# Gates of two branches as seven half-block products, and pooling inputs by way of DRAM

## The chip, the cores and the metric

The kernel runs on one core of a Trainium2 chip. A core has TensorE (PE: matmuls, with a queue of weight loads of its own, PEld), VectorE (DVE), ScalarE (ACT), GpSimd (POOL) and SyncE (SP), whose queue issues all of this kernel's DMAs. The metric is the time of one execution on the device in microseconds (us), the median of several runs.

## The reference

One layer of a streaming encoder over 1152 tokens (1024 of a prompt, 8 x 16 of samples), width 1024, in float32: a gated feed-forward block, a mixer, and a second feed-forward block, each between norms. What matters here is the mixer:

```python
proj = xn @ w_in   # [pooling 512 | z 1024 | x/B/C 2048 | dt 16 | u 512 | v 512 | gates 3*1024]
ya = pool_mixer(xa)            # branch A: trailing-window means of 512 channels
yb = rms_norm(ssd(x, B, C, dt) * silu(z))   # branch B: state-space scan
yc = u * spatial_gate(layer_norm(v))        # branch C
gates = sigmoid(gate_cols)     # three gates of 1024 channels
merged = gates[0] * (ya @ wa) + gates[1] * (yb @ wb) + gates[2] * (yc @ wc)
out = merged @ w_out
```

The gates are thus three products of the normed input (1152 x 1024) with weights of 1024 x 1024, each followed by a sigmoid.

## The kernel before

Tokens are cut into 9 tiles of 128, and these into NCHK = 3 chunks of CH = 384. Channels lie on the 128 partitions. Every float32 operand of a large product is split into a high part (an ACT cast to the type float32r) and a low part (a DVE subtraction: `split`, L123), and each product is three matmuls (low x high, high x low, high x high: `mm3`, L203). `proj` (L209) makes one output tile of 128 channels x 384 tokens with 8 x 3 = 24 matmuls of 384 columns into a PSUM bank. `load_w` (L127) loads one 1024 x 128 weight column block (512 KB) into a staging buffer (three of them) and splits it into one of two buffers `w_hi`, `w_lo`.

The normed input of the mixer is held as `xT[c]`, high and low, for the three chunks. The stages follow each other in `trunk`:

- the first feed-forward block (`gate_up`, then `down`, with `tail`);
- eight units of filler for PE, four of them between the last transposes (L1167 to L1174). The filler is a generator, `gate_out(0)`: it makes gate A one output tile (column block j, chunk c) at a time, chunk 0 first, with a weight load for each, and stores it in DRAM (`gad`). `filler(k)` (L813) takes the next k units;
- `z_dt` (L530): z in four groups of 256 columns, nine tiles each, weights in two buffers (`wz`); the terms of dt behind the second group;
- `branch_c` (L607): loads of its norm vectors, biases and spatial weights (`gn_g`, `gn_b`, `bs`, `ws`: L613 to L627), then v in two halves; one filler unit and the transposes of the spatial weights (`turned`, L628, which begins with DVE's masked copy L630) stand ahead of the second half; then u;
- `branch_a` (L695): four groups of 128 channels. Each computes its pooling input for three chunks (72 matmuls, L722 to L729) into `x`, then sums in up to four steps on DVE and POOL in turn (L737), the difference `zz` (L741), three units of filler (in the last group all that are left, L750), and the group's small product (`pya`, L761);
- `merge_ac` (L775): for each of 8 column blocks j: gate C for three chunks (72 matmuls), multiplied into `acc` with the product of branch C (`pyw`, 36 matmuls); then gate A read back from DRAM (`sa`) and multiplied with the product of branch A (36 matmuls), POOL's sum, and a store to DRAM (`accd`);
- `ssd` (branch B, with gate B as filler), `finish`, the output projection and the second feed-forward block.

The feed-forward blocks already use a scheme with seven half-block products in place of eight (`operands` L263, `weights` L289, `prod` L321, `cell` L328). A 2 x 2 block product, with the input dimension halved and two column blocks against two token blocks, is made from seven products of sums of blocks: `weights` makes seven half blocks of 512 x 128 from two loaded columns with four subtractions on POOL and splits each into a buffer `w2`; `operands` does the like for the tokens; `cell` adds the products with DVE and ACT in PSUM banks and in x and y.

Instructions are put in order by a scheduler at build time: program order is the priority, and an instruction takes its place in its engine's queue, in order, when the scheduler expects its operands and a free buffer. At run time every queue runs strictly in order, SP's too, each instruction waiting for its semaphores. Buffers of a pool are shared out in program order, to whichever is free.

Of the kernel before, what the change touches and what calls it, by code (L numbers as in the profile page):

```python
# [18 lines left out]
P = 128  # L19
D = 1024  # L20
# [41 lines left out]
class Net:  # L62
# [75 lines left out]
    def load_wide(self, pool, w, c0, extra=None):  # L138

        nc = self.nc  # L140
        hi = pool.tile([P, 8, 272], F32R, name="wz_hi")
        lo = pool.tile([P, 8, 272], F32R, name="wz_lo")
# [146 lines left out]
    def weights(self, w, c_left, c_right, wp=None):  # L289

        nc = self.nc
        raw = []
        for c0 in (c_left, c_right):
            r = self.stage("wraw").rearrange("p (k c) -> p k c", k=KD)
            nc.sync.dma_start(r, w[:, c0 : c0 + P].rearrange("(k p) c -> p k c", p=P))
            raw.append(r)
        b11, b21 = raw[0][:, 0:4], raw[0][:, 4:8]
        b12, b22 = raw[1][:, 0:4], raw[1][:, 4:8]
        t1 = self.wtp.tile([P, 4, P], F32, name="wt")
        B = {}  # L300

        def out(name, raw):
            b = (wp or self.wp).tile([P, 2, 4, P], F32R, name="w2")
# [12 lines left out]
        op(b21, b21, t1)  # L316
        out("t4", b21)
        out("22", b22)
        return B

    def prod(self, ps, b, a, first):  # L321
# [173 lines left out]


class Mixer:
    def __init__(self, n, xT, yz_d, zs_d, acc_d, ga_d, gb_d, cum_d, last_d):
        self.n, self.nc, self.tc, self.io, self.xT = n, n.nc, n.tc, n.io, xT
        self.yz_d, self.zs_d, self.acc_d, self.ga_d, self.gb_d, self.cum_d, self.last_d = yz_d, zs_d, acc_d, ga_d, gb_d, cum_d, last_d  # L500
        self.w_in = self.io["w_in"][0]

    def masks(self, pool):
# [23 lines left out]
        self.strict_s = pool.tile([P, P], F32, name="strict_s")  # L527
        nc.gpsimd.tensor_tensor(self.strict_s, self.strict, bd, op=ALU.mult)

    def z_dt(self, pool):  # L530

        n, nc, io = self.n, self.nc, self.io
        dtb = n.spread(pool, io["ssm_dt_bias"][0], "dtb")
        self.dt = pool.tile([P, NT, HEADS], F32, name="dt")
        with self.tc.tile_pool(name="wz", bufs=2) as wz, self.tc.tile_pool(name="zt", bufs=3) as zt:
            for g in range(GROUPS):
                w = n.load_wide(wz, self.w_in, C_Z + 256 * g, C_DT if g == 0 else None)
                nn = 272 if g == 0 else 256
                for t in range(NT):
                    ps = n.psum("pz")  # L540
                    n.proj_tok(ps, t, self.xT, w, nn)
                    z = zt.tile([P, 256], F32, name="z")
                    nc.scalar.activation(z, ps[:, :256], AF.Silu)
                    nc.sync.dma_start(self.zs_d[t * P : (t + 1) * P, 256 * g : 256 * g + 256], z)
                    if g == 0:
                        nc.vector.tensor_tensor(self.dt[:, t, :], ps[:, 256:272], dtb, op=ALU.add)
                if g == 1:
                    self.dt_terms(pool, zt)

    def dt_terms(self, pool, tmp):  # L550
        n, nc, io = self.n, self.nc, self.io
# [52 lines left out]
        nc.vector.tensor_copy(el, tp[:HEADS, P : 2 * P].rearrange("p (b i) -> p b i", i=LSEQ)[:, :, LSEQ - 1])  # L604
        nc.sync.dma_start(self.last_d, el)

    def branch_c(self, pool):  # L607

        n, nc, tc, io = self.n, self.nc, self.tc, self.io
        self.yc = [pool.tile([P, 4, TOK], F32R, name=f"yc{i}") for i in range(2)]  # L610
        with tc.tile_pool(name="cc", bufs=1) as cc, tc.tile_pool(name="ct", bufs=3) as ct:
# [36 lines left out]
            with tc.tile_pool(name="wz", bufs=1) as wz:  # L648
                for half in range(2):
                    w = n.load_wide(wz, self.w_in, C_V + 256 * half)  # L650
                    if half == 1:
                        self.filler(1)
                        turned()
                    for t in range(NT):
                        ps = n.psum("pv")
                        n.proj_tok(ps, t, self.xT, w, 256)
                        nc.scalar.copy(vv[:, t, 256 * half : 256 * half + 256], ps[:, :256])
                        if half == 1:
                            self.layer_norm(ct, vv[:, t, :], gn_g, gn_b)
                            if t == 8:  # L660
                                nc.sync.dma_start(io["gmlp_v_s"][0].rearrange("b s c -> (b s) c"), vv[:, t, :])
# [33 lines left out]
    def branch_a(self, pool):  # L695
# [5 lines left out]
        with tc.tile_pool(name="pa", bufs=1) as pa:  # L701
# [15 lines left out]
            for g in range(4):  # L717
# [1 line left out]
                x = pa.tile([P, RAWP], F32, name="xa")  # L719
                nc.gpsimd.memset(x[:, :POOL_HIST], 0.0)  # L720
                nc.gpsimd.tensor_copy(sample(x)[:, :, :POOL_HIST], hT[:, g])
                for c in range(NCHK):  # L722
                    ps = n.psum("pxa")
                    n.proj(ps, w, self.xT[c])
                    if c < 2:
                        nc.scalar.copy(x[:, POOL_HIST + c * CH : POOL_HIST + (c + 1) * CH], ps[:, :CH])
                    else:
                        nc.scalar.copy(x[:, POOL_HIST + 2 * CH : sb], ps[:, : 2 * P])
                        nc.scalar.copy(sample(x)[:, :, POOL_HIST:], ps[:, 2 * P : CH].rearrange("p (b i) -> p b i", i=LSEQ))  # L729
                win = 2  # L730
                s = x
                for step in range(g + 1):
# [42 lines left out]
    def merge_ac(self):  # L775

        n, nc, tc, io = self.n, self.nc, self.tc, self.io
        with tc.tile_pool(name="mac", bufs=3) as mp, tc.tile_pool(name="macc", bufs=NCHK + 1) as mk:
            for j in range(KD):
                js = slice(j * P, (j + 1) * P)  # L780
                acc = [mk.tile([P, CH], F32, name="acc") for _ in range(NCHK)]
                wg = n.load_w(self.w_in, C_G + 2 * D + j * P, KD)
                wyc = n.load_w(io["w_branch_c"][0], j * P, 4)
                for c in range(NCHK):
                    cs = slice(c * CH, (c + 1) * CH)
                    s = mp.tile([P, CH], F32, name="sg")
                    self.gate(wg, self.xT[c], s)
                    ps = n.psum("pyw")
                    n.proj(ps, wyc, [v[:, :, cs] for v in self.yc], 4)
                    nc.vector.tensor_tensor(acc[c], s, ps[:, :CH], op=ALU.mult)  # L790
                wya = n.load_w(io["w_branch_a"][0], j * P, 4)
                for c in range(NCHK):
                    cs = slice(c * CH, (c + 1) * CH)
                    s = mp.tile([P, CH], F32, name="sa")
                    nc.sync.dma_start(s, self.ga_d[js, cs])
                    ps = n.psum("pyw")
                    n.proj(ps, wya, [v[:, :, cs] for v in self.ya], 4)
                    nc.vector.tensor_tensor(s, s, ps[:, :CH], op=ALU.mult)
                    nc.gpsimd.tensor_tensor(acc[c], acc[c], s, op=ALU.add)
                    nc.sync.dma_start(self.acc_d[js, cs], acc[c])  # L800
# [277 lines left out]
def trunk(ctx, tc, io):  # L1078
# [30 lines left out]
    with ExitStack() as c0:  # L1109
# [44 lines left out]
        with ExitStack() as c1:  # L1154
# [7 lines left out]
                tail(io["ffn1_post_g"][0], 0.5, lambda t: rows(io, t), at(h1), lambda t, h, xn: n.prenorm(t, h, gn, xT, xn)),  # L1162
            )
            m = Mixer(
                n, xT, dram("yz", [TOK, D]), dram("zs", [TOK, D]), dram("acc", [D, TOK]), dram("gad", [D, TOK]), dram("gbd", [D, TOK]), dram("cumd", [NT * HEADS, P]), dram("lastd", [HEADS, NSEQ])
            )
# [105 lines left out]
```

## Time and profile before

| | |
|---|---|
| median of 3 runs | 2885.55 us (2882.87 to 2886.64) |
| profiled execution | 2887.22 us, its span 2885.5 us |
| PE, PEld busy | 2797.2 us, 2635.4 us |
| DVE, ACT, POOL busy | 1366.8, 985.9, 767.3 us |
| DMA | 335.14 MB, mean 116 GB/s |

The span is the profiled part of one execution. An engine is busy while it works on an instruction; busy shares add over stages with different limits, so each stage is looked at by itself. The rows below give for an instruction its line, engine, operation, output and inputs, and in brackets how long its engine was idle before it and what ended that.

### The profile page before, as it was taken

To read this page: it belongs to the slowest core of one execution; us is meant where nothing else is said; L and a number is where in the kernel's file an instruction comes from. 1 tells how busy PE (TensorE), PEld (TensorE's weight loads), DVE (VectorE), ACT (ScalarE), POOL (GpSimd) and SP (SyncE) were. 2 spreads that over 40 slices of the span, in tenths; PEclk is the share of its full clock that TensorE was granted. 3 is DMA by queue.
4 is the path that set the end of the run, shared out by engine and by line. 5 is a ranking of instruction groups with operands and counts; after the bars stand their busy time and mean duration, and the time that the engine had idled before them with its cause. 6 is when DMAs were issued, how large, how long until landed. Compare 5 with 4: busy or idle time off the path is not lost. (4 is left out here: it accounts for less than half of the span.)

```text
span 2885.5 us, 43479 instructions
## 1 busy us (share of the span) xinstructions
PE 2797.2 (97%) x17310; PEld 2635.4 (91%) x17310; DVE 1366.8 (47%) x1989; ACT 985.9 (34%) x1720; POOL 767.3 (27%) x877
## 2 busy tenths in 40 slices
PE   6999999999999999999999999999989999999999
PEld 6999999888889999999998889998789999998887
DVE  7544443445643063322266676544564444445553
ACT  6322222344443112311134446523342222224442
POOL 3443343100010010111146676221233333330000
PEclk9999999999999999999999999999999999999999
DMA  4222221556654113332323446744122222226663
GB/s 128 69 80 77 73 69 55 170 189 212 214 148 133 49 44 92 101 94 86 108 66 101 116 107 176 225 136 152 66 94 81 69 73 70 83 74 220 222 215 108
DMA packets 331463, 335.14 MB, mean 116 GB/s; under 512 B 23150, under 2 KB 285538, under 8 KB 331261
## 3 DMA queue, kind: packets, MB, share of 16 engines
q1 hardware_dynamic: 331261, 332.37, 37.5%
q8 instruction: 136, 2.23, 0.3%
q14 instruction: 66, 0.54, 0.1%
HBM read 263.06 MB, written 69.25 MB: 115 GB/s over the span
## 5 line engine op out<-in xcount | busy, mean ns | idle before, releaser
L324 PE MATMUL pw<-A_s,w 128*128 128x288 f32 x4224 | 607.0, 299 | 17.0 <-ACT A_s L124 8.4
L324 PEld LDWEIGHTS pw<-A_s,w 128*128 128x128 f32 x4224 | 575.5, 191 | 25.0 <-ACT A_s L124 9.1
L206 PE MATMUL down<-wd,hh 128*128 128x512 f32 x2376 | 542.5, 390 | 4.0 <-ACT wd L124 3.1
L206 PEld LDWEIGHTS down<-wd,hh 128*128 128x128 f32 x2376 | 444.9, 188 | 98.5 <-ACT wd L124 4.1
L324 PE MATMUL pw<-A,w 128*128 128x288 f32 x3168 | 452.5, 296 | 8.1 <-DVE A L125 5.2
L324 PEld LDWEIGHTS pw<-A,w 128*128 128x128 f32 x3168 | 433.0, 190 | 9.3 <-DVE A L125 5.4
L206 PE MATMUL pgate<-xT,w_hi 128*128 128x384 f32 x1152 | 295.6, 338 | 0.0
L125 DVE TENSOR_TENSOR w<-wraw,w 128x512 fp32r<-128x512 f32 x220 | 180.4, 822 | 130.3 <-ACT w L124 130.0
L125 DVE TENSOR_TENSOR wd<-wdraw,wd 128x1024 fp32r<-128x1024 f32 x140 | 172.5, 1236 | 127.5 <-ACT wd L124 127.1
L206 PEld LDWEIGHTS pgate<-xT,w_hi 128*128 128x128 f32 x1152 | 209.4, 189 | 0.4
L206 PE MATMUL pgate<-xT,w_lo 128*128 128x384 f32 x576 | 196.9, 342 | 9.4 <-DVE w_lo L125 9.4
L206 PE MATMUL pxbc<-xT,w_hi 128*128 128x384 f32 x768 | 199.0, 339 | 0.0
L124 ACT CAST wd<-wdraw 128x1024 fp32r<-128x1024 f32 x140 | 146.6, 1051 | 141.9 <-PE down L206 90.6
L125 DVE TENSOR_TENSOR w_lo<-wraw,w_hi 128x1024 fp32r<-128x1024 f32 (+1 forms) x104 | 127.4, 1225 | 123.2 <-ACT w_hi L124 110.5
L124 ACT CAST w<-wraw 128x512 fp32r<-128x512 f32 x220 | 135.6, 619 | 62.3 <-PE pw L324 32.6
L163 POOL TENSOR_SCALAR post_r<-post_ss 128x1 f32<-128x1 f32 x27 | 8.3, 306 | 552.5 <-ACT junk L174 552.5
L375 POOL TENSOR_TENSOR wh<-wh,wy 128x288 f32<-128x288 f32 x88 | 82.3, 936 | 234.3 <-ACT wh L364 169.4
L206 PEld LDWEIGHTS pxbc<-xT,w_hi 128*128 128x128 f32 x768 | 140.8, 191 | 0.1
L206 PE MATMUL pxbc<-xT,w_lo 128*128 128x384 f32 x384 | 133.7, 348 | 0.0
L124 ACT CAST w_hi<-wraw 128x1024 fp32r<-128x1024 f32 (+1 forms) x104 | 102.4, 985 | 85.9 <-PE pyw L206 45.9
L349 ACT ACTIVATE wh<-pw 128x288 f32<-128x288 f32 x88 | 36.2, 411 | 276.2 <-PE pw L324 275.7
L341 DVE TENSOR_TENSOR wx<-wx,pw 128x288 f32<-128x288 f32 x176 | 79.7, 453 | 100.2 <-PE pw L324 99.6
(281 smaller groups left out, 4249.6 us busy)
## 6 DMA issues: line engine op xcount, KB each, us to landing
wdraw<-in_ffn_w_down_dram SPq DMA_DIRECT2D x132, 512.0 KB
wraw<-in_ffn_w_gu_dram SPq DMA_DIRECT2D x88, 512.0 KB
wraw<-in_w_in_dram SPq DMA_DIRECT2D x80, 512.0 KB
hff<-wh SPq DMA_DIRECT2D x88, 288.0 KB
hr<-hff SPq DMA_DIRECT2D x132, 192.0 KB
h<-fg SPq DMA_DIRECT2D x18, 512.0 KB
cumb<-cumd SPq DMA_DIRECT2D x36, 256.0 KB
h<-h SPq DMA_DIRECT2D x18, 512.0 KB
```

The lines of the kernel that those rows point to most:

```text
L124: self.last_hi = self.nc.scalar.copy(hi, raw)
L125: return (eng or self.nc.vector).tensor_tensor(lo, raw, hi.bitcast(F32), op=ALU.subtract)
L163: nc.gpsimd.tensor_scalar(r, ss[0], ss[1], eps, op0=ALU.add, op1=ALU.add)
L206: mm = self.nc.tensor.matmul(ps, lhsT=lhs[a], rhs=rhs[b], start=first and i == 0, stop=last and i == 2)
L324: self.nc.tensor.matmul(ps[:, :HCH], lhsT=b[:, x, k], rhs=a[:, y, k], start=first and k == 0 and i == 0, stop=k == 3 and i == 2, skip_grou ...
L341: nc.vector.tensor_tensor(o, i, b[k][:, :HCH], op=ALU.add)
L349: nc.scalar.activation(h[:, 0], b[2][:, :HCH], AF.Silu)
L375: nc.gpsimd.tensor_tensor(h[:, 1], h[:, 1], y, op=ALU.mult)
```

## The change

Gates A and C are no longer made as filler and in the merge. For chunks 0 and 1 they are made together, in a stage of their own between z and branch C, as eight pairs: column block j of gate A and column block j of gate C are the two columns, chunks 0 and 1 the two token blocks, and each pair takes seven products of 12 matmuls with 384 columns (`pair`). The sums of token blocks are made once, on POOL, in buffers of the pool `aux` (five in all), and split (`sums`). Both gates go to DRAM. The third chunk of both gates is the new filler of branches C and A (`gates_last`, 16 units, each with a weight load). The pooling inputs of chunks 0 and 1 become the filler behind the first feed-forward block (`xa_out`, 8 units with 4 weight loads) and go through DRAM; branch A computes only chunk 2 and loads the rest. Branch C takes two more units of filler ahead of v. The merge reads gate C from DRAM. The z weights alternate between two pools, one of which makes room for four buffers of the pairs' weights (`Wa`); the other three are in `Wb`. z goes through the pool `act` (three buffers).

```diff
     def prod(self, ps, b, a, first, n=HCH):
...
-                    ps[:, :HCH], lhsT=b[:, x, k], rhs=a[:, y, k], start=first and k == 0 and i == 0, stop=k == 3 and i == 2, skip_group_check=not first
+                    ps[:, :n], lhsT=b[:, x, k], rhs=a(y, k), start=first and k == 0 and i == 0, stop=k == 3 and i == 2, skip_group_check=not first
...
-    def z_dt(self, pool):
+    def z_dt(self, pool, sp, cg):
...
-        with self.tc.tile_pool(name="wz", bufs=2) as wz, self.tc.tile_pool(name="zt", bufs=3) as zt:
+        with self.tc.tile_pool(name="wzb", bufs=1) as wzb, self.tc.tile_pool(name="zt", bufs=3) as zt:
+            ca = ExitStack()
+            wza = n.pool(ca, "wza", 1, "right")
             for g in range(GROUPS):
-                w = n.load_wide(wz, self.w_in, C_Z + 256 * g, C_DT if g == 0 else None)
+                if g == 3:
+                    ca.close()
+                    wa = n.pool(cg, "Wa", 4, "right")
+                w = n.load_wide((wza, wzb)[g % 2], self.w_in, C_Z + 256 * g, C_DT if g == 0 else None)
+                if g == 2:
+                    self.sums(sp)
...
+    def sums(self, pool):
...
+        self.S = {k: pool.tile([P, 2, 4, CH], F32R, name=f"S{k}") for k in ("s1", "s3", "s2", "s4")}
+        for kp in range(2):
+            raw = {}
+            for t in range(2):
+                for k in range(2):
+                    ks = slice(4 * k + 2 * kp, 4 * k + 2 * kp + 2)
+                    r = raw[t, k] = n.aux("sraw")[:, : 2 * CH].rearrange("p (k c) -> p k c", k=2)
+                    nc.gpsimd.tensor_tensor(r, x[t][0][:, ks].bitcast(F32), x[t][1][:, ks].bitcast(F32), op=ALU.add)
...
+            def out(name, dst, a, b, op):
+                nc.gpsimd.tensor_tensor(dst, a, b, op=op)
+                n.split(dst, self.S[name][:, 0, ks], self.S[name][:, 1, ks])
...
+    def pair(self, c_left, c_right, left, right, wp):
...
+        B = n.weights(self.w_in, c_left, c_right, wp)
+        xy = n.aux("gw")
+        x, y = xy[:, :CH], xy[:, 512 : 512 + CH]
...
+        def put(ps, add, dst, c):
+            s = n.actp.tile([P, CH], F32, name="sgo", tag="act")
+            if add is None:
+                nc.scalar.activation(s, ps[:, :CH], AF.Sigmoid)
+            else:
+                nc.vector.tensor_tensor(s, add, ps[:, :CH], op=ALU.add)
+                nc.scalar.activation(s, s, AF.Sigmoid)
+            nc.sync.dma_start(dst[:, c * CH : (c + 1) * CH], s)
+
+        b1 = prod("11", "11")
+        nc.scalar.copy(x, b1[:, :CH])
+        b = prod("t2", "s2")
+        nc.vector.tensor_tensor(x, x, b[:, :CH], op=ALU.add)
+        b = prod("t3", "s3")
+        nc.vector.tensor_tensor(y, x, b[:, :CH], op=ALU.add)
+        b5 = prod("t1", "s1")
+        put(b5, y, right, 1)
+        put(prod("t4", "22"), y, left, 1)
+        prod("21", "12", b1)
+        put(b1, None, left, 0)
+        prod("22", "s4", b5)
+        put(b5, x, right, 0)
+
+    def gates_ac(self, wa, wb):
+        for j in range(KD):
+            js = slice(j * P, (j + 1) * P)
+            self.pair(C_G + j * P, C_G + 2 * D + j * P, self.ga_d[js], self.gc_d[js], lambda k: wa if k in ("11", "t1", "t2", "t3") else wb)
...
     def branch_c(self, pool):
...
                     w = n.load_wide(wz, self.w_in, C_V + 256 * half)
+                    if half == 0:
+                        self.filler(2)
...
     def branch_a(self, pool):
...
-                for c in range(NCHK):
-                    ps = n.psum("pxa")
-                    n.proj(ps, w, self.xT[c])
...
+                nc.sync.dma_start(x[:, POOL_HIST : POOL_HIST + 2 * CH], self.xa_d[g * P : (g + 1) * P])
+                ps = n.psum("pxa")
+                n.proj(ps, w, self.xT[2])
...
     def merge_ac(self):
...
-                wg = n.load_w(self.w_in, C_G + 2 * D + j * P, KD)
...
-                    self.gate(wg, self.xT[c], s)
+                    nc.sync.dma_start(s, self.gc_d[js, cs])
...
-            m.fill, m.filled = m.gate_out(0, m.ga_d), 0
+            m.fill, m.filled = m.xa_out(), 0
...
-            m.z_dt(mixc)
+            with tc.tile_pool(name="S", bufs=1) as sp, tc.tile_pool(name="wt", bufs=1) as n.wtp, ExitStack() as cg:
+                wa = m.z_dt(mixc, sp, cg)
+                m.gates_ac(wa, n.pool(cg, "Wb", 3))
+            m.fill, m.filled = m.gates_last(), 0
```

## Rows read from the trace of the kernel before

**Rows 1.** The page: busy time of the engines, and GB/s in 40 slices of the span.

```profile
PE 2797.2 (97%) x17310; PEld 2635.4 (91%) x17310; DVE 1366.8 (47%) x1989; ACT 985.9 (34%) x1720; POOL 767.3 (27%) x877
...
GB/s 128 69 80 77 73 69 55 170 189 212 214 148 133 49 44 92 101 94 86 108 66 101 116 107 176 225 136 152 66 94 81 69 73 70 83 74 220 222 215 108
```

**Rows 2.** The waits of PE from 820 to 1640 us.

```profile
PE pgate L206 <- DVE w_lo L125: 4.6, 4, 1.6
...
PE wsT L640 <- DVE ws L630: 3.8, 1, 3.8
```

**Rows 3.** PE's timeline where the fillers after the first stage wait longest.

```profile
848.23 0.44 PE L206 MATMUL pgate<-xT,w_lo 128*128 128x384 f32 x1 [1.59 <-DVE w_lo L125]
```

**Rows 4.** PE in windows around 1008 us: us, busy (count), clock, DMA, GB/s.

```profile
1008.00:1012.00 4.00, 2.78 (x11) 0.57 0.06 7
...
1012.00:1016.00 4.00, 4.00 (x23) 0.58 0.96 275
```

**Rows 5.** SP's timeline from 940 to 1010 us, its loads for branch C.

```profile
977.30 0.33 SPq L485 DMA_DIRECT2D gn_g<-in_gmlp_norm_g_dram  x1
...
978.62 16.51 SPq L618 DMA_DIRECT2D bs<-in_gmlp_bs_dram  x4
...
995.18 11.04 SPq L627 DMA_DIRECT2D ws<-in_gmlp_ws_dram  x8
```

**Rows 6.** Busy time in windows: us, then PE, PEld, DVE, ACT, POOL, clock, DMA, GB/s.

```profile
870.00:980.00 110.00, 110.00 (x917) 109.98 (x916) 20.90 (x48) 30.69 (x56) 0.00 (x0) 1.00 0.35 103
...
1230.00:1430.00 200.00, 200.00 (x1155) 199.53 (x1154) 46.94 (x71) 30.59 (x49) 28.64 (x27) 1.00 0.32 93
...
2530.00:2700.00 170.00, 169.32 (x987) 152.51 (x986) 86.04 (x121) 65.77 (x110) 28.97 (x29) 1.00 0.49 155
...
2700.00:2860.00 160.00, 160.00 (x708) 132.48 (x707) 76.91 (x93) 59.53 (x89) 3.46 (x8) 1.00 0.61 198
```

**Rows 7.** PE's timeline in the second gate and up stage, two cells of 84 products.

```profile
2160.70 4.92 PE L324 MATMUL pw<-A_s,w 128*128 128x288 f32 x36
...
2171.92 4.92 PE L324 MATMUL pw<-A_s,w 128*128 128x288 f32 x36
```

**Rows 8.** Groups by line: count, busy us, mean ns, idle time before and its releaser.

```profile
L125 DVE TENSOR_TENSOR w<-wraw,w 128x512 fp32r<-128x512 f32 x220 | 180.4, 822 | 130.3 <-ACT w L124 130.0
...
L124 ACT CAST w<-wraw 128x512 fp32r<-128x512 f32 x220 | 135.6, 619 | 62.3 <-PE pw L324 32.6 <-POOL wraw L307 28.3 <-DMA wraw<-in_ffn_w_gu_dram 1.4
...
L307 POOL TENSOR_TENSOR wraw<-wraw 128x512 f32<-128x512 f32 x44 | 67.2, 1528 | 2.1
...
L737 POOL TENSOR_TENSOR sum<-sum 128x1284 f32<-128x1284 f32 (+1 forms) x4 | 13.4, 3355 | 6.0 <-DVE sum L737 6.0
...
L790 DVE TENSOR_TENSOR acc<-sg,pyw 128x384 f32<-128x384 f32 x24 | 13.3, 554 | 88.1 <-PE pyw L206 88.1
...
L773 ACT ACTIVATE sgo<-pgate 128x384 f32<-128x384 f32 x48 | 23.5, 490 | 91.2 <-PE pgate L206 91.0
```

**Rows 9.** The timeline where one cell's last products free buffers for the next weights.

```profile
2150.02 0.63 ACT L124 CAST w<-wraw 128x512 fp32r<-128x512 f32 x1
...
2151.33 0.62 ACT L124 CAST w<-wt 128x512 fp32r<-128x512 f32 x1 [0.68 <-PE pw L324]
...
2160.50 0.38 SPq L295 DMA_DIRECT2D wraw<-in_ffn_w_gu_dram  x1
...
2161.03 0.81 POOL L376 TENSOR_TENSOR wh<-wh,wx 128x288 f32<-128x288 f32 x1 [1.16 <-DVE wx L341]
...
2161.20 1.18 DVE L125 TENSOR_TENSOR w<-wraw,w 128x512 fp32r<-128x512 f32 x1 [0.25 <-ACT w L124]
...
2164.38 1.29 POOL L307 TENSOR_TENSOR wt<-wraw 128x512 f32<-128x512 f32 x1 [2.54 <-DMA wraw<-in_ffn_w_gu_dram]
```

**Rows 10.** DVE's timeline at the third group of branch A.

```profile
1165.85 1.61 DVE L737 TENSOR_TENSOR sum<-xa 128x1286 f32<-128x1286 f32 x1 [9.63 <-ACT xa L729]
...
1174.99 1.23 DVE L125 TENSOR_TENSOR w_lo<-wraw,w_hi 128x1024 fp32r<-128x1024 f32 x1
```

More of the change, by code (lines that the diff above doesn't have):

```diff
@@ L140, in load_wide @@
         nc = self.nc
-        hi = pool.tile([P, 8, 272], F32R, name="wz_hi")
-        lo = pool.tile([P, 8, 272], F32R, name="wz_lo")
+        nn = 256 if extra is None else 272
+        hi = pool.tile([P, 8, nn], F32R, name="wz_hi")
+        lo = pool.tile([P, 8, nn], F32R, name="wz_lo")
         for half in range(2):
@@ L302, in out @@
         def out(name, raw):
-            b = (wp or self.wp).tile([P, 2, 4, P], F32R, name="w2")
+            b = (wp(name) if callable(wp) else wp or self.wp).tile([P, 2, 4, P], F32R, name="w2")
             self.split(raw, b[:, 0], b[:, 1])
@@ L319, in weights, with prod @@
         return B
-    def prod(self, ps, b, a, first):
+    def prod(self, ps, b, a, first, n=HCH):
+        a = a if callable(a) else lambda y, k, a=a: a[:, y, k]
         for k in range(4):
@@ L541, in z_dt @@
                     n.proj_tok(ps, t, self.xT, w, nn)
-                    z = zt.tile([P, 256], F32, name="z")
+                    z = n.actp.tile([P, CH], F32, name="z", tag="act")[:, :256]
                     nc.scalar.activation(z, ps[:, :256], AF.Silu)
@@ L548, in z_dt @@
                     self.dt_terms(pool, zt)
+        return wa
     def dt_terms(self, pool, tmp):
@@ L605, in dt_terms @@
         nc.sync.dma_start(self.last_d, el)
+    def sums(self, pool):
+        n, nc, x = self.n, self.nc, self.xT
+        self.S = {k: pool.tile([P, 2, 4, CH], F32R, name=f"S{k}") for k in ("s1", "s3", "s2", "s4")}
[6 more added lines that the diff above has]
+                    nc.gpsimd.tensor_tensor(r, x[t][0][:, ks].bitcast(F32), x[t][1][:, ks].bitcast(F32), op=ALU.add)
+            ks = slice(2 * kp, 2 * kp + 2)
+            def out(name, dst, a, b, op):
+                nc.gpsimd.tensor_tensor(dst, a, b, op=op)
+                n.split(dst, self.S[name][:, 0, ks], self.S[name][:, 1, ks])
+            out("s1", raw[1, 1], raw[1, 0], raw[1, 1], ALU.add)
+            out("s3", raw[1, 0], raw[0, 0], raw[1, 0], ALU.subtract)
+            out("s2", raw[1, 1], raw[1, 1], raw[0, 0], ALU.subtract)
+            out("s4", raw[0, 1], raw[0, 1], raw[1, 1], ALU.subtract)
@@ new lines, in pair, with prod @@
+    def pair(self, c_left, c_right, left, right, wp):
+        n, nc, xT = self.n, self.nc, self.xT
+        A = {k: (lambda y, i, v=v: v[:, y, i]) for k, v in self.S.items()}
+        A["11"] = lambda y, k: xT[0][y][:, k]
+        A["12"] = lambda y, k: xT[0][y][:, 4 + k]
+        A["22"] = lambda y, k: xT[1][y][:, 4 + k]
+        B = n.weights(self.w_in, c_left, c_right, wp)
+        xy = n.aux("gw")
+        x, y = xy[:, :CH], xy[:, 512 : 512 + CH]
+        def prod(w, v, bank=None):
+            ps = n.psum("pw") if bank is None else bank
+            n.prod(ps, B[w], A[v], bank is None, CH)
+            return ps
+        def put(ps, add, dst, c):
[19 more added lines that the diff above has]
+        put(b5, x, right, 0)
@@ new lines, in gates_ac, with gates_last @@
+    def gates_ac(self, wa, wb):
+        for j in range(KD):
+            js = slice(j * P, (j + 1) * P)
+            self.pair(C_G + j * P, C_G + 2 * D + j * P, self.ga_d[js], self.gc_d[js], lambda k: wa if k in ("11", "t1", "t2", "t3") else wb)
+    def gates_last(self):
+        n, nc = self.n, self.nc
+        for i, dst in ((0, self.ga_d), (2, self.gc_d)):
+            for j in range(KD):
+                wg = n.load_w(self.w_in, C_G + i * D + j * P, KD)
+                s = n.actp.tile([P, CH], F32, name="sgo", tag="act")
+                self.gate(wg, self.xT[2], s)
+                nc.sync.dma_start(dst[j * P : (j + 1) * P, 2 * CH :], s)
+                yield
@@ L607, in branch_c, with xa_out @@
+    def xa_out(self):
+        n, nc = self.n, self.nc
+        for g in range(4):
+            w = n.load_w(self.w_in, C_XA + P * g, KD)
+            for c in range(2):
+                ps = n.psum("pxa")
+                n.proj(ps, w, self.xT[c])
+                s = n.actp.tile([P, CH], F32, name="sgo", tag="act")
+                nc.scalar.copy(s, ps[:, :CH])
+                nc.sync.dma_start(self.xa_d[g * P : (g + 1) * P, c * CH : (c + 1) * CH], s)
+                yield
     def branch_c(self, pool):
@@ L721, in branch_a @@
                 nc.gpsimd.tensor_copy(sample(x)[:, :, :POOL_HIST], hT[:, g])
-                for c in range(NCHK):
-                    ps = n.psum("pxa")
-                    n.proj(ps, w, self.xT[c])
[L725 to L729, printed above, removed]
+                nc.sync.dma_start(x[:, POOL_HIST : POOL_HIST + 2 * CH], self.xa_d[g * P : (g + 1) * P])
+                ps = n.psum("pxa")
+                n.proj(ps, w, self.xT[2])
+                nc.scalar.copy(x[:, POOL_HIST + 2 * CH : sb], ps[:, : 2 * P])
+                nc.scalar.copy(sample(x)[:, :, POOL_HIST:], ps[:, 2 * P : CH].rearrange("p (b i) -> p b i", i=LSEQ))
                 win = 2
@@ L1164, in trunk @@
             m = Mixer(
-                n, xT, dram("yz", [TOK, D]), dram("zs", [TOK, D]), dram("acc", [D, TOK]), dram("gad", [D, TOK]), dram("gbd", [D, TOK]), dram("cumd", [NT * HEADS, P]), dram("lastd", [HEADS, NSEQ])
+                n, xT, dram("yz", [TOK, D]), dram("zs", [TOK, D]), dram("acc", [D, TOK]), dram("gad", [D, TOK]), dram("gbd", [D, TOK]), dram("gcd", [D, TOK]), dram("xad", [POOL_W, 2 * CH]), dram("cumd", [NT * HEADS, P]), dram("lastd", [HEADS, NSEQ])
             )
-            m.fill, m.filled = m.gate_out(0, m.ga_d), 0
+            m.fill, m.filled = m.xa_out(), 0
             for _ in range(4):
```

4 lines of the change are left out of this document (2 added, 2 removed).

## Prediction

> **What bounds the kernel now.** I read the page's busy times first: TensorE (PE) is busy for 97% of the span, VectorE (DVE) for 47%, ScalarE (ACT) for 34% and GpSimd (POOL) for 27% [rows 1]. So the time is the sum of PE's matmuls plus PE's own idle, and only these two can change it. Then the waits of PE alone, over the stages that the change touches, 820 to 1640 us: PE waited there for weights of the gates (pgate, four times, 4.6 us in all, the longest 1.6) and once 3.8 us for DVE's masked copy of the spatial weights (wsT, for ws) [rows 2]. The longest of the four is at 848 us, where the gates of branch A run as filler straight behind the first feed-forward stage and need a fresh weight for each 24 matmuls [rows 3]; the other three, 3.0 us, are therefore elsewhere, in branch A. The 3.8 us wait costs more than itself: in the 8 us after 1008 us the granted clock is 0.57 and 0.58 [rows 4], so most of that time went at 1.2 GHz instead of 2.4 GHz. The lost part is (1 - 0.57) x 2.78 + (1 - 0.58) x 4.00 = 2.9 us. Its cause is read on SP's queue: the loads of branch C start at 977.3 us, four issues of bs take 16.5 us, and the eight of ws end only at 995.18 + 11.04 = 1006.2 us [rows 5].
>
> **The products.** Before, gates A and C of chunks 0 and 1 take 2 branches x 8 column blocks x 2 chunks x 24 = 768 matmuls of 384 columns. After, each of the 8 block pairs takes 7 products of 12: 672 matmuls, also of 384 columns. The last chunk (2 x 8 x 24 = 384) and the pooling inputs (288) keep their counts. So 96 matmuls go. One costs 200.00 / 1155 = 0.173 us where PE does nothing but such matmuls [rows 6]: **-16.6 us**, all on the path.
>
> Is a matmul of a block product dearer? The feed-forward stage does the same products, with 288 columns: from one row of 36 to the next, one cell of 84, are 11.22 us, 0.134 each [rows 7]. That is 0.014 over the 0.120 that 288 columns take at 2.4 GHz, and 0.173 is 0.013 over the 0.160 of 384 columns, so no. A pair should last 84 x 0.173 = 14.5 us.
>
> **Weights of the pairs.** Each pair splits seven half blocks instead of two whole weights: 7 x 0.62 us on ACT, 7 x 0.82 on DVE, four subtractions of up to 1.53 on POOL. Its evictions are five DVE adds like the 0.55 of L790, one ACT copy and four sigmoids at 0.49 [rows 8]. That makes DVE 7 x 0.82 + 5 x 0.55 = 8.5 us, ACT about 6.8, POOL 6.1, each below the 14.5 of PE. The order matters more than the sum, since there is one set of seven buffers. In the feed-forward stage, also with seven buffers, ACT's casts of the next set come at 2150.02 and 2151.33, the second right after PE frees a buffer, while PE still has products of the old cell to do; and raw weights issued at 2160.50 are used by POOL at 2164.38 [rows 9]. In a pair the next set's first four buffers (11, t1, t2, t3) come free with its first four products, 8.3 us after its start, and 6.2 us remain. Bounds per pair: nothing (those cells), and 0.55 + 0.49 + 0.62 + 1.18 = 2.84 us if the next set waited for the last eviction, its sigmoid, a cast and a split at the dearest value of rows 9. I take 0.3 x 8 = **+2.4 us**, near the rows that do the same work.
>
> That 1.18 us is a split against a mean of 0.82, with a POOL operation of 0.81 started 0.17 before it [rows 8, 9]. The Trainium skill, page "SBUF — State Buffer", section "Who interferes with whom", says why: a DVE instruction with two SBUF inputs and a GpSimd instruction that reads SBUF exclude each other for a whole instruction, so the change, which puts POOL work beside DVE splits in two more stages, would make splits late. This trace agrees in that place. By the rule in its strictest form a split could first wait out a subtraction of 1.53, and the handover above would cost 0.55 + 0.49 + 0.62 + 1.53 + 0.82 = 4.0 us in place of 2.84: eight of them bring the sum to 2895 us where the rows bring it to 2865.
>
> **The operand sums.** Sixteen POOL operations of 768 elements, 1.53 us for 512 and 3.36 for 1284 [rows 8], so about 2.1 each, 34 us; eight casts and eight splits of at most 0.93 and 1.23 us (1.5 times those of 512). They stand with the third z group. From 870 to 980 us POOL is idle and DVE and ACT are busy for 20.9 and 30.7 of 110 us [rows 6], and two z groups of 216 matmuls at 0.12 us are 52 us long. Hidden; 18 us are to spare. If the cover went, the first pair would wait up to 34 us.
>
> **Moved fillers.** The eight fillers behind the feed-forward stage become pooling inputs: the same matmuls, but one weight for two chunks, four loads and splits in place of eight. The 1.6 us wait at 848 us [rows 3] should go: **-1.6**, with 0 as the other bound.
>
> Two fillers now stand ahead of the first half of v: 2 x 24 x 0.173 = 8.3 us between the start of branch C, where its loads are freed, and its use of ws. The loads were late by 3.8 us, so the wait and the slow clock behind it go: **-6.7**. The other bound is 0, or a like loss if a filler's weight is queued behind the 16.5 us of bs on SP. For the two hand-overs (z to pairs, pairs to branch C) I take one wait of the kind of rows 3, **+1.6**, between 0 and 3.8.
>
> **Branch A and the merge.** Branch A loses 48 of 72 matmuls of each group to the earlier filler, so a group lasts 4.2 + 12.5 us and the last 4.2 + 16.6. Behind the pooled input, DVE's chain runs from the first sum at 1165.85 to the split at 1174.99, 9 us [rows 10], inside the 12.5 us of three fillers; the fourth sum step of the last group adds 3.4 and stays inside 16.6. A filler's split still queues behind that chain, so the 3.0 us in three waits stay: 0, between -3 and +4. The input's load must wait for the old one's last reader, and is needed 4.2 us later, about the 3.9 of the load in rows 9.
>
> The merge now reads both gates: per column block 512 KB of weights, 1152 KB of gates and 576 KB of stores in 72 x 0.173 = 12.5 us, 184 GB/s. In the last stage 198 GB/s go by with PE busy for 160 of 160 us at a DMA share of 0.61 [rows 6], while the slices of the touched stages show 44 to 133 [rows 1]. SP has 11 issues of 0.4 us per block. The acc store waits on SP for POOL, with the next block's loads behind it; these are due 12.5 us later. I take 0, with 3 as the upper bound. The other DMAs (writing gates C and pooling inputs, four more weight loads) lie beside work with an idle queue. All other stages keep their work: 0.
>
> **Sum.** The profiled execution took 2887.2 us: -16.6 + 2.4 - 1.6 - 6.7 + 1.6 = -20.9, so 2866.3. The median of the runs, 2885.55, is 1.7 lower, which gives **2865 us**.
>
> **Rivals.** *The ws wait stays or another of its size takes its place* (SP's order puts a filler's load behind bs): 6.7 back, 2872 us. For it: rows 5 show how long SP can be blocked. Against: the extra 8.3 us. Chance 0.25.
>
> *Each pair waits for its weights: slower.* Place: the first product of a pair, on DVE's split of 11. Price: 2.84 us of wait, and if each brings the clock down as after 1008 us [rows 4] another 2.9, so 5.7 x 8 = 46 us, 2865 - 2.4 + 46 = 2909 us; without the clock 2885. It decides the sign from 3 us a pair, (20.9 + 2.4) / 8. For it: one set of buffers, ACT's and DVE's queues in order, the last sigmoid ahead of the next cast. Against: rows 9. Chance 0.07. The Trainium skill, page "TensorE: Matmul & The Clock Gate", section "HAM oscillation — how this bites in real kernels", describes such a gap paid again in each turn of a loop; the one long gap in these stages agrees with it.
>
> *The merge becomes bound by DMA*: if it got only the 155 GB/s of 2530 to 2700 us [rows 6], a block would take 14.8 us, 8 x 2.3 = 18 us more, 2883 us. For it: rows of 1.5 KB and 512 B. Against: 198 GB/s beside a full PE. Chance 0.04.
>
> *The change does not do what it says*: the products start late, because POOL begins the sums only when z is done (a buffer that is not free) and its 34 us are exposed: 2865 + 34 = 2899 us. For it: five shared buffers, of which the sums want four. Against: nothing else asks for them in z. Chance 0.05.
>
> **Numbers.** The forecast has 0.59. Its own range is 2858 (branch A's waits and both of my allowances gone) to 2869. With the first rival, 0.84 lies in 2857 to 2880, which also takes in the bounds of the merge and of branch A. A measurement of this kernel tells 0.2%, 5.8 us, from no change. Faster: forecast and first rival, 0.84. Same: the merge, 0.04. Slower: the waiting pairs and the exposed sums, 0.12.
>
> **What would show it.** Right: 96 fewer matmuls; pw rows of 384 columns in eight blocks of 14.5 us each, with no wait for DVE's splits; no wait at 848 us and none of wsT, the clock at 1.00 through the v projection; the merge at 12.5 us a block. Wrong: PE waits named w or S in the pairs, sg in the merge, or SP held by bs while a filler's weight is due. A time above 2880 us means that one of these is there eight times.

## The result, and the profile after

The changed kernel takes 2902.42 us (median of 4 runs, 2898.37 to 2908.30) against 2886.10 us before (4 runs, 2882.87 to 2887.76): a ratio of 1.0053 [1.0039, 1.0068]. It is **16 us slower**, where 20 us less were forecast and 2880 was the upper end. The profiled execution took 2898.37 us, its span 2896.6 us, 11.1 us over the span before.

The page's busy times of the kernel after, which answer to [rows 1]:

```profile
PE 2782.7 (96%) x17214; PEld 2617.3 (90%) x17214; DVE 1430.3 (49%) x2081; ACT 1011.1 (35%) x1778; POOL 843.7 (29%) x925
```

The 96 matmuls are gone, and PE is busy for 14.5 us less. So the loss is PE's idle time: its share fell from 97% to 96%. The waits of PE from 820 to 1640 us, which answer to [rows 2]:

```profile
PE pxa L207 <- DVE w_lo L125: 15.0, 2, 13.4
PE pv L207 <- ACT vv L759: 10.2, 1, 10.2
PE pw L326 <- DVE sgo L660: 5.5, 6, 2.6
...
PE pgate L207 <- DVE w_lo L125: 3.1, 3, 1.6
```

wsT is not in the list any more, and the three small waits of branch A stayed, as forecast. Three new ones of some size came, one in each stage that the change filled (a fourth, of 1.3 us, is for the split behind a transpose among the fillers). To see what each costs with the slow clock behind it, I took each stage from its first instruction on PE to the first of the next stage, as the table shows. "Repaired" is the last experiment below.

| stretch on PE, us | before | after | repaired |
|---|---|---|---|
| eight fillers, up to z | 37.1 | 54.7 | 35.3 |
| z | 105.4 | 105.6 | 105.6 |
| eight pairs | none | 124.3 | 117.0 |
| two fillers ahead of v | none | 8.5 | 8.5 |
| v with its filler, up to u | 64.4 | 69.1 | 56.7 |
| u, branch A and merge | 387.1 | 246.9 | 246.5 |

From branch A and the merge 141.3 us of matmuls were to go (576 of gate C, 192 of the pooling inputs and two fillers' 48, at 0.173), and 140.2 went. The loss is in the fillers (+17.7), in v (+4.8) and in the pairs (124.3 against 8 x 14.55 = 116.4).

**The fillers.** PE's timeline between 845 and 885 us has these two stops:

```profile
857.17 0.44 PE L207 MATMUL pxa<-xT,w_lo 128*128 128x384 f32 x1 [1.67 <-DVE w_lo L125]
...
879.11 0.69 PE L207 MATMUL pxa<-xT,w_lo 128*128 128x384 f32 x1 [13.36 <-DVE w_lo L125]
```

The releaser is DVE's split of the filler's weight. DVE, ACT and POOL ahead of it, each engine's timeline in a fence of its own:

```profile
876.24 2.82 DVE L125 TENSOR_TENSOR w_lo<-wraw,w_hi 128x1024 fp32r<-128x1024 f32 x1
```

```profile
859.58 0.47 ACT L703 COPY sgo<-pxa 128x384 f32<-128x384 f32 x1
870.03 0.83 ACT L124 CAST Ss<-sraw 128x768 fp32r<-128x768 f32 x1 [9.98 <-POOL sraw L631]
...
873.03 1.05 ACT L124 CAST w_hi<-wraw 128x1024 fp32r<-128x1024 f32 x1
```

```profile
833.98 1.83 POOL L627 TENSOR_TENSOR sraw<-xT,xT 128x768 f32<-128x768 f32 x1 [1.45 <-DVE h L189]
...
858.78 9.35 POOL L627 TENSOR_TENSOR sraw<-xT,xT 128x768 f32<-128x768 f32 x4
868.20 3.69 POOL L631 TENSOR_TENSOR sraw<-sraw 128x768 f32<-128x768 f32 x2
```

The operand sums are not with the third z group, where program order has them. They begin at 833.98 us, beside the eight fillers. Their operands, chunks 0 and 1, had been there since about 757 us; the row's releaser, DVE's L189, reads `fg`, a buffer of the same pool `aux`, so by the kernel it is this buffer that they waited for. ACT's queue has the cast of a sum ahead of the cast of the last filler's weight. POOL finishes that sum only at about 870 us, ACT stands still for 9.98 us, and the weight's cast starts at 873.03 us. DVE's queue has sums' splits ahead of the weight's too. The clock then makes it dearer: it falls during the stop, and in the 11 us behind it its mean is 0.81, so a part of them went at 1.2 GHz in place of 2.4. PE in windows, with its busy time and its granted clock (the sixth group):

```profile
865.00:879.00 14.00, 0.75 (x5) 0.43 (x3) 8.11 (x6) 5.76 (x8) 11.85 (x6) 0.66 0.09 19
879.00:890.00 11.00, 10.89 (x53) 10.89 (x54) 5.58 (x7) 4.59 (x8) 0.00 (x0) 0.81 0.78 231
```

**Branch C.** SP's timeline, which answers to [rows 5]:

```profile
1124.84 15.32 SPq L718 DMA_DIRECT2D bs<-in_gmlp_bs_dram  x4
1140.21 11.10 SPq L727 DMA_DIRECT2D ws<-in_gmlp_ws_dram  x8
...
1152.35 17.88 SPq L132 DMA_DIRECT2D wraw<-in_w_in_dram  x5
```

The weight of a filler, wraw of L132, stands on SP behind bs and ws. ACT's and PE's timelines show who was queued behind it:

```profile
1130.77 0.37 ACT L759 COPY vv<-pv 128x256 f32<-128x256 f32 x1 [2.28 <-PE pv L207]
1156.44 1.04 ACT L124 CAST w_hi<-wraw 128x1024 fp32r<-128x1024 f32 x1 [25.30 <-DMA wraw<-in_w_in_dram]
1157.39 0.64 ACT L759 COPY vv<-pv 128x256 f32<-128x256 f32 x2
```

```profile
1157.81 0.58 PE L207 MATMUL pv<-wz_hi,xT 128*128 128x256 f32 x1 [10.18 <-ACT vv L759]
```

ACT's queue has the cast of that weight between the first and the second eviction of v. It waits for the load for 25.30 us, v's evictions wait behind it, and PE runs out of free PSUM banks. The weight itself is not due yet: its filler runs only ahead of the second half.

**The pairs.** The third pair is typical. PE's seventh product waits for DVE's eviction of L660; the four fences are PE, DVE, ACT and POOL around it:

```profile
1041.04 0.45 PE L326 MATMUL pw<-Ss,w 128*128 128x384 f32 x1 [2.62 <-DVE sgo L660]
```

```profile
1036.55 1.23 DVE L125 TENSOR_TENSOR w<-wt,w 128x512 fp32r<-128x512 f32 x1 [3.15 <-ACT w L124]
...
1039.82 0.69 DVE L125 TENSOR_TENSOR w<-wt,w 128x512 fp32r<-128x512 f32 x1 [1.58 <-ACT w L124]
1040.43 0.55 DVE L660 TENSOR_TENSOR sgo<-gw,pw 128x384 f32<-128x384 f32 x1
```

```profile
1035.89 0.62 ACT L124 CAST w<-wt 128x512 fp32r<-128x512 f32 x1 [3.69 <-POOL wt L308]
...
1039.17 0.62 ACT L124 CAST w<-wt 128x512 fp32r<-128x512 f32 x1 [2.66 <-POOL wt L308]
```

```profile
1034.58 1.28 POOL L308 TENSOR_TENSOR wt<-wraw 128x512 f32<-128x512 f32 x1 [5.71 <-DMA wraw<-in_w_in_dram]
```

The seventh product (22 with s4) accumulates into the bank of the fourth, b5, so it waits until b5's gate has been taken out, by an addition that stands on DVE behind two splits of the next pair's t1 and t2. These wait for ACT, ACT for POOL, and POOL for the load of the right raw column (L296). The wait is thus not for weights of its own product but for an eviction behind the next pair's weights.

### The profile page after: what moved, and what is told of

It is laid out like the page before. It is cut to its first block, busy times and chain, and to the rows that moved or that the text cites. A ratio compares the mean times of both kernels' runs of the same rounds, so it can differ in the third digit from the quotient of the medians.

```text
span 2896.6 us, 43750 instructions
## 1 busy us (share of the span) xinstructions
PE 2782.7 (96%) x17214; PEld 2617.3 (90%) x17214; DVE 1430.3 (49%) x2081; ACT 1011.1 (35%) x1778; POOL 843.7 (29%) x925
## 5 line engine op out<-in xcount | busy, mean ns | idle before, releaser
L125 DVE TENSOR_TENSOR w<-wraw,w 128x512 fp32r<-128x512 f32 x260 | 207.8, 801 | 195.9 <-ACT w L124 195.0
L124 ACT CAST w<-wraw 128x512 fp32r<-128x512 f32 x260 | 159.1, 618 | 72.2 <-POOL wraw L308 39.4
L207 PE MATMUL pgate<-xT,w_hi 128*128 128x384 f32 x640 | 164.1, 337 | 0.0
L125 DVE TENSOR_TENSOR w_lo<-wraw,w_hi 128x1024 fp32r<-128x1024 f32 (+1 forms) x92 | 114.0, 1240 | 79.6 <-ACT w_hi L124 71.6
L124 ACT CAST w_hi<-wraw 128x1024 fp32r<-128x1024 f32 (+1 forms) x92 | 89.9, 978 | 157.2 <-PE pyw L207 84.5
L343 DVE TENSOR_TENSOR wh<-wy,pw 128x288 f32<-128x288 f32 x88 | 39.9, 454 | 182.4 <-PE pw L326 182.4
L308 POOL TENSOR_TENSOR wraw<-wraw,wt 128x512 f32<-128x512 f32 x52 | 67.7, 1302 | 208.6 <-DVE w L125 202.2
```

What stands on the lines that cost most here:

```text
L124: self.last_hi = self.nc.scalar.copy(hi, raw)
L125: return (eng or self.nc.vector).tensor_tensor(lo, raw, hi.bitcast(F32), op=ALU.subtract)
L207: mm = self.nc.tensor.matmul(ps, lhsT=lhs[a], rhs=rhs[b], start=first and i == 0, stop=last and i == 2)
L343: nc.vector.tensor_tensor(o, i, b[k][:, :HCH], op=ALU.add)
```

## The experiments

The kernel before ran beside them on the same chip: 2884.31 us (23 runs) for the first four, 2885.41 us (25 runs) for the last four. All ratios are to it. "Under the change" is the difference to the 2902.42 us of the result; no run of the changed kernel beside the experiments is on record, and the kernel before took 1.8 and 0.7 us less here than beside the result, so these differences are uncertain by about as much.

**e1: the sums tied to z.** A POOL copy that reads the last z tile of the second group stands ahead of the sums, so that they can't be moved up: they run beside the third group.

```diff
                 if g == 2:
-                    self.sums(sp)
+                    mark = pool.tile([P, 1], F32, name="mark")
+                    with self.tc.issue_after(nc.gpsimd.tensor_copy(mark, z[:, :1]).ins):
+                        self.sums(sp)
```

> The changed kernel with POOL's sixteen sums queued behind one small POOL copy that reads the last z tile of the second group, so that they run beside the third group. Theory: the sums were put ahead, beside the eight filler units, and the casts and splits of their results stand in ACT's and DVE's queues ahead of the weights of the last filler units, so that PE waits 13.4 us for them. Then the stretch from the first filler unit to z falls from 54.7 us to about 37, as before the change, and the time from 2902 to about 2884 us (2880 to 2889). Rival: the filler's own weight loads are late, four loads behind each other; then the wait of over 10 us stays at the last units, and the time at 2902.

Measured: 2888.53 us, 1.0017 [1.0008, 1.0026]. The fillers' stretch fell from 54.7 to 35.3 us, all of its loss and 1.8 us under before. But z grew from 105.6 to 116.9 us, which was not expected, though the time lies in the expected range. A row of PE's waits and four of ACT's timeline in e1:

```profile
PE pz L207 <- ACT z L554: 8.1, 2, 7.4
```

```profile
943.47 0.38 ACT L554 ACTIVATE z<-pz 128x256 f32<-128x256 f32 x1
951.37 0.83 ACT L124 CAST Ss<-sraw 128x768 fp32r<-128x768 f32 x1 [7.53 <-POOL sraw L633]
953.25 0.83 ACT L124 CAST Ss<-sraw 128x768 fp32r<-128x768 f32 x1 [1.05 <-POOL sraw L633]
953.99 0.38 ACT L554 ACTIVATE z<-pz 128x256 f32<-128x256 f32 x1
```

So it is the same fault in another stage: ACT stands for 7.53 us at a cast whose sum POOL has not made, with z's activation behind it. The place that the prediction assumed is no cover either, although POOL has the time there. What must be covered is not POOL's 34 us but every wait for POOL in the queues of ACT and DVE.

**e2: a short load of bs.** The four loads of bs, each 1024 rows of 64 bytes, become one load of the 16 values for four heads and four POOL copies.

```diff
+            bq = cc.tile([P, GH_G, LSEQ], F32, name="bq")
+            nc.sync.dma_start(bq, io["gmlp_bs"][0:1, :, :LSEQ].broadcast_to([P, GH_G, LSEQ]))
             for h in range(GH_G):
-                nc.sync.dma_start(
-                    bs[:, 1, h].rearrange("p (b i) -> p b i", i=LSEQ),
-                    io["gmlp_bs"][0, h : h + 1, :LSEQ].unsqueeze(1).broadcast_to([P, NSEQ, LSEQ]),
-                )
+                nc.gpsimd.tensor_copy(bs[:, 1, h].rearrange("p (b i) -> p b i", i=LSEQ), bq[:, h].unsqueeze(1).broadcast_to([P, NSEQ, LSEQ]))
```

> The changed kernel with the four loads of bs for the sample tokens (15 us on SP) replaced by one small load and four POOL copies. Theory: PE's 10.2 us wait in the v projection comes from SP: the weight of the next filler unit is issued behind bs and ws, ACT's cast of it stands ahead of the evictions of v, and PE runs out of PSUM banks. With SP free some 15 us earlier the wait goes, the stretch from v to u falls from 69.1 to about 57 us, and the time from 2902 to about 2890 us. Rival: the evictions of v are late by themselves, or it is ws and not bs that holds SP; then the wait of about 10 us stays and the time at 2902.

Measured: 2887.06 us, 1.0011 [1.0002, 1.0020], 15.4 us under the change. From v to u it is 56.7 us, and the wait for vv is gone. SP's timeline in e2:

```profile
1123.15 0.49 SPq L718 DMA_DIRECT2D bq<-in_gmlp_bs_dram  x1
1123.68 6.11 SPq L726 DMA_DIRECT2D ws<-in_gmlp_ws_dram  x8
```

The 15.32 us of bs are 0.49 now, and ws, issued behind it, takes 6.11 in place of 11.10. The filler's weight comes early, and the order on ACT, which is as before, does no harm. So a short bs is enough: the two fillers need not go. Whether moving the cast behind v's evictions would be enough too was not run.

**e3: a bank of its own for the seventh product.** Its bank is a fresh one, and b5 is added to x on DVE.

```diff
-        prod("22", "s4", b5)
-        put(b5, x, right, 0)
+        nc.vector.tensor_tensor(x, x, b5[:, :CH], op=ALU.add)
+        put(prod("22", "s4"), x, right, 0)
```

> The changed kernel with the seventh product of a pair in a PSUM bank of its own, added by one DVE operation more, where it was accumulated into the bank of the fourth. Theory: PE's waits in the pairs (5.5 us in six of eight) are for DVE's eviction of the fourth product out of that bank, which stands in DVE's queue behind splits of the next weights; with a bank of its own they go, the pairs fall from 124.3 to about 118 us and the time from 2902 to about 2897. Rival: the weights of the next pair are late anyway; then the waits move to another product, the pairs stay at 123 us or more and the time at 2902.

Measured: 2901.07 us, 1.0056 [1.0043, 1.0069]: no gain. Two waits of PE in e3:

```profile
PE pgate L207 <- DVE w_lo L125: 6.4, 5, 1.6
PE pw L326 <- DVE w L125: 1.4, 3, 0.7
```

The waits for sgo are gone, but PE now waits for the weights (w, 1.4 us) and in both fillers behind the pairs (pgate has two waits more, 3.3 us). From the first pair to v it is 131.4 us, against 132.8. The bank was only the place where the lateness showed: the weights themselves come too slowly.

**e4: all three.**

> All three edits together. Theory: the three waits are independent, so the gains add up: 2902 - 18 - 12 - 5 = about 2867 us (2862 to 2873), 0.6% below the kernel before. Rival: a wait removed comes back at the next place, because DVE, ACT or SP is late for a reason that all three share; then the time stays above 2878 us.

Measured: 2874.83 us, 0.9965 [0.9954, 0.9977]. It is faster than before, but above what was expected. Its three main waits of PE name what is left, e1's cost in z and the weights' rate of e3:

```profile
PE pz L207 <- ACT z L554: 7.4, 1, 7.4
PE pgate L207 <- DVE w_lo L125: 6.0, 5, 1.6
PE pw L326 <- DVE w L125: 3.9, 5, 1.7
```

**e5: the sums on DVE.** If the place beside the fillers were bad in itself, faster sums there would not help; if the fault is that POOL makes them too slowly for the order of the queues, they would.

```diff
-                    nc.gpsimd.tensor_tensor(r, x[t][0][:, ks].bitcast(F32), x[t][1][:, ks].bitcast(F32), op=ALU.add)
+                    nc.vector.tensor_tensor(r, x[t][0][:, ks].bitcast(F32), x[t][1][:, ks].bitcast(F32), op=ALU.add)
...
-                nc.gpsimd.tensor_tensor(dst, a, b, op=op)
+                nc.vector.tensor_tensor(dst, a, b, op=op)
```

> The changed kernel with the sixteen sums on DVE instead of POOL, at the same early place beside the filler. A sum takes POOL 1.83 to 2.5 us there; DVE's split of the same 768 elements takes 1.8 with POOL beside it and should take about 1.0 alone. Theory: the early place hurts only because POOL is late (and makes DVE's splits wait), so that casts and weights queued behind the results wait; with 16 us of sums on DVE instead of 34 on POOL the stretch from the filler to z falls from 54.7 to 36 to 40 us, z stays at 105.5, and the time goes from 2902 to about 2886 us. Rival: it is the place alone, work ahead of the last weights on whichever engine; then the stretch stays above 46 us and the time above 2893.

Measured: 2881.44 us, 0.9988 [0.9979, 0.9997], 21.0 us under the change. The fillers' stretch is 35.3 us, as in e1, and z 105.6, without e1's loss. DVE's timeline in e5:

```profile
851.74 0.95 DVE L627 TENSOR_TENSOR sraw<-xT,xT 128x768 f32<-128x768 f32 x1
...
853.48 0.95 DVE L125 TENSOR_TENSOR Ss<-sraw,Ss 128x768 fp32r<-128x768 f32 x1
...
856.50 1.22 DVE L125 TENSOR_TENSOR w_lo<-wraw,w_hi 128x1024 fp32r<-128x1024 f32 x1
```

The sixteen sums take 0.95 to 1.21 us each in place of POOL's 1.80 to 2.90. The split of a weight takes 1.22 us, where it took 2.82 beside POOL's subtraction. DVE is busy for 33.71 of the 37 us from 833 us on, and PE for all of them. The place was fine for an engine that keeps up. The run does not tell apart POOL's own slowness and the slowing of DVE's splits beside it, since it takes away both.

**e7: raw buffers of their own for the left column of a pair.** In the change, each pair's raw columns come from the three staging buffers `wraw`. The left column is held until the split of t4, which is made in it, near the end of the set. With three buffers for two columns a pair, the next pair's right column has to wait for this one's left buffer: SP issues it at 1030.27 us, and POOL's subtraction at 1034.58, shown above, waits for it. The load at 1031.77 us, into the buffer that the split of 22 frees, is the left column of the pair after that. The next right column follows at 1045.67 us, a round of 15.4 us against 14.55 of products. SP's timeline of the change:

```profile
1030.27 0.38 SPq L296 DMA_DIRECT2D wraw<-in_w_in_dram  x1
...
1031.77 0.38 SPq L296 DMA_DIRECT2D wraw<-in_w_in_dram  x1
...
1045.67 0.38 SPq L296 DMA_DIRECT2D wraw<-in_w_in_dram  x1
```

```diff
-            r = self.stage("wraw").rearrange("p (k c) -> p k c", k=KD)
+            r = (lp.tile([P, 1024], F32, name="wrawl") if lp and not raw else self.stage("wraw")).rearrange("p (k c) -> p k c", k=KD)
...
-                m.gates_ac(wa, n.pool(cg, "Wb", 3))
+                m.gates_ac(wa, n.pool(cg, "Wb", 3), n.pool(cg, "Lr", 2))
```

(The pool is handed on to `weights` as `lp`, from the second pair on.)

> The changed kernel with two raw buffers of their own for the left weight column of the pairs, in space that is free then; the right column and all else keep the three shared ones. Theory: a pair lasts 15.4 us because raw weights go round: a column is loaded when the split of t4 of the pair before frees its buffer, then load, difference, cast, split and again to t4; DVE's evictions stand behind these splits. With two buffers more the next columns are loaded a pair ahead, the waits of 5.5 us go, the pairs fall from 124.3 to about 118 us and the time from 2902 to 2896. Rival: the chain over POOL, ACT and DVE itself is as long as a pair; then the pairs stay at 123 us or more.

Measured: 2891.09 us, 1.0025 [1.0015, 1.0035], 11.3 us under the change. From the first pair to v it is 125.5 us, 7.3 less, and the eight pairs alone last 117.0 us. PE's largest waits in e7:

```profile
PE pxa L207 <- DVE w_lo L125: 13.5, 2, 11.8
PE pv L207 <- ACT vv L759: 7.5, 1, 7.5
PE pgate L207 <- DVE w_lo L125: 3.1, 3, 1.6
```

No wait of pw is left, though the seventh product still shares its bank. What e3 moved, e7 removed: the chain began at the staging buffers. The vv wait shrank too, from 10.2 to 7.5 us, which the pairs' stretch does not hold.

**e8: the short bs in the kernel before.** How much of e2's gain belongs to the change?

> The kernel before with only the short load of bs. Theory: its own 3.8 us wait for ws and the 2.9 us of slow clock behind it come from the same 16.5 us on SP and go: 2884.3 - 6.7 = about 2878 us. Rival: the eight loads of ws are late by themselves; then the wait and the time stay.

Measured: 2878.95 us, 0.9980 [0.9971, 0.9989], 6.5 us under the kernel before. From v to u it is 57.0 us in place of 64.4, and of [rows 2] only this is left:

```profile
PE pgate L206 <- DVE w_lo L125: 4.6, 4, 1.6
```

The forecast's 6.7 us for the wait for wsT and the slow clock behind it was thus right in size; it did not need the two fillers.

**e10: e2, e5 and e7 together.**

> The changed kernel with sums on DVE, the short load of bs and the two raw buffers of the pairs. Theory: 2902 - 16 - 12 - 6 = about 2868 us (2863 to 2873), z without the wait of 7.4 us that the later sums on POOL brought, and below the 2874.8 of the three edits together. Rival: a wait comes back elsewhere and the time stays above 2874.

Measured: **2859.93 us** (4 runs, 2858.25 to 2863.41), 0.9916 [0.9902, 0.9929], below what was expected and faster than both kernels. Of PE's waits from 820 to 1340 us one row is left, and over the eight pairs PE is busy throughout (windows, 974 to 1092 us):

```profile
PE pgate L207 <- DVE w_lo L125: 3.1, 3, 1.6
```

```profile
974.00:1092.00 118.00, 118.00 (x681) 118.00 (x681) 68.87 (x96) 55.35 (x97) 40.26 (x29) 1.00 0.45 137
```

The three parts alone gave 15.4, 21.0 and 11.3 us, 47.7 in sum; together they gave 42.5. Part of the difference is the 2.7 us of the vv wait that e7 and e2 both count. Beside e8, which has the short bs too, the change with its other two faults mended is worth 2878.95 - 2859.93 = 19.0 us.

## Why the prediction was wrong

By its own terms, in the profiled executions (stages of the table above):

| term | forecast | after | repaired (e10) |
|---|---|---|---|
| products: branch A and merge, 116.4 of pairs, two fillers | -16.6 | -15.3 | -15.7 |
| pairs' weights, beyond 116.4 | +2.4 | +7.9 | +0.6 |
| fillers behind the first stage | -1.6 | +17.7 | -1.8 |
| v, with its wait and its slow clock | -6.7 | +4.8 | -7.7 |
| two hand-overs | +1.6 | 0 | 0 |
| sum | -20.9 | +15.1 | -24.6 |

The spans differ by +11.1 and -29.0; the other 4 us of each lie in stages without an edit, mostly the state-space scan, which lasted from 446.6 to 454.0 us in the profiles of all runs.

- **Products: right.** A product of 12 lasts its 2.1 us wherever nothing is waited for, and e10's eight pairs last 117.0 us. The wait of 1.6 us allowed for the two hand-overs did not come.
- **The operand sums: the step that failed.** "They stand with the third z group ... Hidden" was wrong twice. They stand beside the fillers, since an instruction takes its place when the scheduler expects its operands and a free buffer; the text of the kernel's order said so, and the prediction took program order. And the cover was counted as free time of POOL (34 us of 52) and not by who is queued behind the dependent casts on ACT and the splits on DVE. POOL's work was sized right: its sixteen sums took 34.0 us. The splits were not: put at 1.23 us at most, six of the eight took 1.81 to 2.61 us, all while POOL made sums, where a split alone takes 0.95. The prediction had priced splits late beside POOL work only for the pairs. e1 shows that the place named would have cost 11 us in z; e5 shows that the early place costs nothing if the sums come in time (in z, faster sums were not run). That the scheduler took POOL for faster than it is is only argued, from the order that it made.
- **The rival of exposed sums** gave 2899 us, close to the result, for another reason: "POOL begins the sums only when z is done" is the opposite of what the trace shows, so its nearness is luck.
- **Branch C: the first rival's mechanism, at another price.** The wait for wsT went, as forecast. "SP's order puts a filler's load behind bs" came true, but with 6.7 us as its price, the loss returning. In fact v lasts 11.5 us more than forecast (4.8 longer than before in place of 6.7 shorter), because the load's cast held the evictions of v on ACT. The prediction asked what is queued behind the load on SP, not what is queued behind its cast on ACT.
- **The pairs: right place, wrong size.** 7.9 us lie between the bounds of 0 and 8 x 2.84 = 22.7, and 2.4 was chosen from the cells of [rows 9]. What failed is the assumed release: the next set's first buffers were free in time, but the raw columns were not, as e7 shows. The waits never reached the rival's 3 us in each pair, and the clock stayed at 1.00 there, so its 46 us did not come.
- **Branch A and the merge: right.** The merge ran with PE busy all the time beside 192 GB/s, so the rival that makes it DMA-bound is out. The windows of the kernel after:

```profile
1340.00:1440.00 100.00, 100.00 (x568) 99.73 (x567) 38.88 (x66) 10.88 (x17) 26.44 (x23) 1.00 0.64 192
```

The range failed with the chances: 0.05 for late sums and 0.25 for a blocked SP were each near what happened, but the one was priced apart from the other, and both came. The last sign, that a time above 2880 us means a wait that "is there eight times", failed too: the largest loss is one wait of 13.4 us in one place.

## What to carry to other kernels

Work is hidden only if everything queued behind its consumers is hidden too: for each added step follow its result to the in-order queues where it is cast, split or evicted, and ask what critical instruction stands behind it there, in the order of the built program and not of the source. A slow helper engine with idle time is no cover when two other engines wait for it in the midst of their critical work; here DVE at 91% busy was the better place. When a wait vanishes and the time does not (e3), the lateness came from further up; follow it back to the transfer or buffer that paces the round.

## What was not expected of the hardware

Four DMA issues of 1024 rows of 64 bytes held SP for 15.32 us, and the eight issues of ws behind them took 11.10 us instead of 6.11 (in the kernel before 11.04 us, and 4.96 in e8): here small rows cost the issues behind them as well. Removing them was worth 6.5 us in the kernel before and 15.4 in the changed one.

Sums on POOL and splits on DVE slow each other. A sum alone takes POOL 1.80 to 1.85 us, and its split alone takes DVE 0.95. From 857 to 865 us DVE makes three splits beside the sums at 858.78 us shown above, and each split takes 2.60 us and each of the first three sums 2.54 to 2.57; the fourth sum, with DVE idle, takes 1.80. DVE's timeline of the change:

```profile
857.03 7.65 DVE L125 TENSOR_TENSOR Ss<-sraw,Ss 128x768 fp32r<-128x768 f32 x3
```

DVE's split of a weight takes 2.82 us beside a subtraction, and 1.22 with POOL idle. The Trainium skill, page "SBUF — State Buffer", section "Who interferes with whom", says that a DVE instruction with two SBUF inputs contends with a GpSimd instruction that reads SBUF, and that the ports they share are an exclusive lock. These rows agree with it: each of the three takes nearly the time of a sum and a split together. In e5 and e10, where POOL makes no sums, the splits take 0.95 and 1.22 us.
